# A decoder layer with a sixth raw weight tile, sums and forms placed elsewhere, norm vectors in SyncE's queue, and classical pair steps bank by bank

## The chip, the core and the metric

One core of a Trainium2 chip runs the whole layer. The metric is the device time of one execution in microseconds (us), lower is better. The kernel before has a median of 1880.06 us over three runs (1879.97 to 1880.45).

## The reference, cut to what matters

The layer has 256 rows and a width of 2048, all in float32. Three token mixers read one projection, their outputs are gated and merged, and a SwiGLU block follows.

```python
h = rms_norm(x, g_pre_mix)
proj = h @ w_in                                  # 2048 x 17488, split into 12 parts
o_a = dsa_attention(...)                         # 64 chosen keys of 256
o_b = retention(...)
o_c = memory_attention(..., rms_norm(mem, g_mem) @ w_mem_kv)
mixed = sum over branches of sigmoid(gate) * (o @ w_branch)
x = x + rms_norm(mixed @ w_out, g_post_mix)
h2 = rms_norm(x, g_pre_ffn)
f_gate, f_up = split(h2 @ w_ffn_in)              # 2048 x 11264
x = x + rms_norm((silu(f_gate) * f_up) @ w_ffn_out, g_post_ffn)
```

## The kernel before, in words

**Weights.** Nearly all work is matrix products of 256 rows with weights from HBM. A `Load` is a raw weight tile of 128 x 4 x 512 float32 (1 MB), fetched by SyncE's queue (SP, L427) into a pool `wr` of `Stream.RAWS` = 5 tiles. Each half of it is an `Item`: ScalarE (ACT) rounds it to float32r (`whi`, L432), VectorE (DVE) makes the remainder (`wlo`, L438), and TensorE (PE) multiplies three times: whi with hi, wlo with hi, whi with lo (L507; `hi` and `lo` are the rounded operand and its remainder). A unit of a normal `Job` is 12 such matmuls, all 512 columns wide; two PSUM banks, one for each half of the rows, are written in turn, three matmuls at a time.

**Order.** `Stream.run` writes the order of the whole program by hand, with no scheduler: before each unit s it issues loads whose first item is at most s + 6 (as long as no more than `RAWS` tiles are in use), casts up to s + 3, remainders up to s + 2, and then the unit's matmuls. Each engine runs its own list in the order in which it was written. Evacuations go into a `fast` list, other side work into a `slow` list, and each unit lets one step of each run (`tick`).

**Pairs.** 19 times two neighbouring products with the same operand are done as a `Pair`: 8 in the gates, merges and `w_out`, 8 in the feed-forward block's first product, and 3 chunks of one pair in `w_ffn_out`. A pair replaces some of its products by a Strassen-like step of seven blocks (each one block = 6 matmuls into one bank, half a unit), and does the rest classically. Its steps are written as `152d3ddd6dd7ccc4ccc` (a shorter string in the last chunk): digits are blocks, `c` and `d` are classical units of the first and the second product. The first product has the banks W and X, the second Y and V. Block 7 is written into X, and `take_7` copies it out with the sign turned (ACT, L313; in the second and third chunk DVE, L315) before X is used for the first `c` step, whose matmuls alternate W, X, W, X. Blocks 5, 6, 7 and 4 need weight sums: the first is a DVE addition of two raw tiles (`t1`, L275; a `Sum` that `add_up` places at most 6 items ahead), the others are accumulating transfers on GpSimd's queue (POOL, L271). Blocks with operand sums read `fhi` and `flo`, which `make_forms` makes from hi and lo (its DVE addition `whole`, an ACT cast, and the remainder at L743); for the retention output `ob` it is put into the slow list at the fourth `values` (i == 3).

**Side transfers.** `turned` transposes an activation through HBM: 8 transfers `d<-y` (L681), then one `turned<-d` (L685), all in SP's queue between the weight loads. Norm vectors (`gain`, 128 x 512, the same row on every partition) come by `bcast` on POOL's queue (L1217); `load_x` fetches a part of x on SP, then two gains, which DVE uses at L1234 and L1236. Side tiles come from the pools `tp` (31 tiles of type T) and `hp` (8 of type H).

Of the kernel before, what the change touches and what calls it, by code (L numbers as in the profile page):

```python
# [19 lines left out]
P = 128  # L20
# [130 lines left out]
class Unit:  # L151


    def __init__(self, s, muls, ready, weight=1.0, begin=None, end=None):
        self.s, self.muls, self.ready, self.weight = s, muls, ready, weight
        self.begin, self.end = begin, end


class Stream:


    RAWS = 5

# [94 lines left out]
    def plan_pair(self, pr):  # L258
# [82 lines left out]
        def plain(g, c, hf, ends):  # L341
            l = loads[g, c]
            s = self.add_item([l], 512, lambda: l.half(hf))
            pair = [acc[a] for a in ("WX", "YV")[g]]

            def stat(m):
                return lambda q: [t[c][:, 2 * hf + q, m * P:(m + 1) * P] for t in (xop.hi, xop.lo)]

            def begin():
                for a in pair:  # L350
                    self.begin(a)

            def end():
                for k in ends:
                    finish(k)
            self.add_unit(Unit(s, [(pair[m], stat(m)) for m in range(2)],
                               lambda: all((c, m) in xop.ready for m in range(2)), begin=begin,
                               end=end if ends else None))

# [81 lines left out]
    def run(self, jobs):  # L441
# [4 lines left out]
        where = {id(l): i for i, l in enumerate(loads)}  # L446
        srcs, his, los = [], [], []
        loaded, summed, added, passed = 0, 0, 0, 0.0

        def add_up():  # L450

            nonlocal summed
            if summed == len(self.sums):
                return False
            t = self.sums[summed]
            if t.after >= len(los) or any(where[id(l)] >= loaded for l in t.loads):
                return False
            t.fn()
            summed += 1
            return True  # L460

        for n, unit in enumerate(self.units):
            s = unit.s
            more = True
            while more:
                more = False
                while loaded < len(loads) and loads[loaded].first <= s + 6:
                    if sum(l.last >= len(los) for l in loads[:loaded]) >= (3 if loaded < 8 else self.RAWS):
                        break
                    self.load(loads[loaded], (4, 2, 2, 2)[loaded] if loaded < 4 else 1)  # L470
                    loaded += 1
                while added < len(self.adds) and self.adds[added].after < len(los):
# [22 lines left out]
            if summed < len(self.sums) and self.sums[summed].before <= s + 6:  # L495
                add_up()
            if unit.begin:
                unit.begin()
            self.until(unit.ready)
            hi, lo = his[s], los[s]  # L500
            for q in range(2):
                for a, parts in unit.muls:
                    xh, xl = parts(q)
                    for x, w in ((xh, hi), (xh, lo), (xl, hi)):
                        held = unit.end is not None and q == 1 and w is hi and x is xl
                        a.n += 1
                        PE.matmul(a.tile, x, w[:, q], start=a.n == 1,  # L507
                                  stop=a.n == a.total or held, skip_group_check=a.read)
            if unit.end:
# [10 lines left out]
def tile_layer(ctx: ExitStack, tc: tile.TileContext, io):  # L520
# [3 lines left out]
    const = ctx.enter_context(tc.tile_pool(name="const", bufs=1))  # L524
    tp = ctx.enter_context(tc.tile_pool(name="tp", bufs=31))
    hp = ctx.enter_context(tc.tile_pool(name="hp", bufs=8))
# [284 lines left out]

    def pair(rows=in_T):

        two = jobs.pop()
        jobs.append(Pair(jobs.pop(), two, rows))
# [372 lines left out]
    def values(i):  # L1188
        def evac(ps):
            tmp = []  # L1190
            yield from copied(tmp, "rv", "x")(ps)
            st.slow.append(retain(i, tmp[0]))
            if i == 3:
                st.slow.append(make_forms(ob, 0))
        return evac
# [19 lines left out]
    def bcast(src, i, n="gain"):  # L1215
        t = H([P, 512], n)
        G.dma_start(t, bass.AP(tensor=src.tensor, offset=src.offset + 512 * i, ap=[[0, P], [1, 512]]))  # L1217
        return t
# [177 lines left out]
    def ffn_up(j):  # L1396
        def evac(ps):
            if j == NF - 1:
                st.slow += [make_forms(act, c) for c in (0, 4, 8)]
            t = ffn.pop(j)  # L1400
            for m in range(2):
                V.scalar_tensor_tensor(t[m], ps[m], rmt["ffn", m], t[m], op0=ALU.mult, op1=ALU.mult)
                yield "free" if m else None
            yield
            turned(t, split_turned(act))
        return evac

    for j in range(NF):
        jobs.append(Job(h2, io["w_ffn_in"][2 * j], KD, 512, ffn_gate(j), lead="" if j else "first"))
        jobs.append(Job(h2, io["w_ffn_in"][2 * j + 1], KD, 512, ffn_up(j)))  # L1410
        if j in BLOCKS:
            pair(lambda g: (in_T if g else in_H)(g))

# [9 lines left out]
    def fin_evac(i):  # L1423
        def evac(ps):
            gt = bcast(io["g_post_ffn"], i)
            if i == 1:
                for k in kept:
                    xr.append(T([P, 2, 512], n="xr"))
                    nc.sync.dma_start(xr[-1], k)
                yo3["g"] = bcast(io["g_post_ffn"], 3)  # L1430
            yo3[i] = T([P, 2, 512], n="yo3")
            yield
# [110 lines left out]
```

## Time and profile before

| | |
|---|---|
| median of 3 runs | 1880.06 us (1879.97 to 1880.45) |
| the profiled execution | 1882.16 us, of which the span from first to last instruction is 1880.4 |
| PE, busy | 1861.9 us (99%), 8330 matmuls |
| PEld (PE's weight loads), busy | 1533.2 us (82%) |
| DVE, busy | 1241.9 us (66%) |
| ACT, busy | 938.7 us (50%) |
| POOL, busy | 75.7 us (4%) |
| HBM read | 411 MB, 229 GB/s over the span |

The span is that of the core's instructions; the profiled execution is 1.8 us longer than it, since it also counts what lies before the first and behind the last. PE's busy time is that of overlapping matmuls: one is shown with 0.39 us, while the next starts 0.23 us later. A short wait is therefore read from the distance of two starts, and a wait shown in brackets, which counts from the modelled end, is short by 0.39 - 0.23 = 0.16 us.

### The profile page before, as it was taken

How to read it: one execution, taken by the hardware profiler on the slowest of the kernel's cores; microseconds unless marked ns; L12 is line 12 of the kernel's file. 1: busy time of each engine (PE TensorE's matmuls, PEld its weight loads, DVE VectorE, ACT ScalarE, POOL GpSimd, SP SyncE). 2: the span in 40 equal slices, each digit the busy share in tenths (PEclk: the TensorE clock that was granted, in tenths of full speed). 3: DMA queues.
4: the chain of work that ended last, by engine and by line, in shares of the span. 5: the costliest groups of instructions: out<-in, count | busy, mean ns of one | idle time of the engine just before them, and what ended most of it. 6: DMA issues, size and time to landing. Idle time of an engine off the chain costs nothing.

```text
span 1880.4 us, 21857 instructions
## 1 busy us (share of the span) xinstructions
PE 1861.9 (99%) x8330; PEld 1533.2 (82%) x8330; DVE 1241.9 (66%) x1509; ACT 938.7 (50%) x1111; POOL 75.7 (4%) x98
## 2 busy tenths in 40 slices
PE   9999999999999999999999999999999999999998
PEld 6888878888888888888887887888888888887886
DVE  5766767777656654556777676756767676666664
ACT  7744444545545444444555444545555555445442
POOL 0000000000000000000100000000000000000000
PEclk9999999999999999999999999999999999999999
DMA  9847565547676756555668684578888887577782
GB/s 372 307 164 265 209 241 188 183 177 247 216 243 217 226 207 221 192 196 189 211 218 296 213 280 157 208 233 286 275 272 257 258 248 244 186 262 226 238 291 84
DMA packets 106201, 432.59 MB, mean 230 GB/s; under 512 B 12000, under 2 KB 43232, under 8 KB 64624
## 3 DMA queue, kind: packets, MB, share of 16 engines
q1 hardware_dynamic: 96720, 398.12, 57.3%
q0 software_dynamic: 9232, 33.07, 10.1%
q8 instruction: 65, 1.06, 0.2%
q14 instruction: 40, 0.33, 0.0%
q10 hardware_dynamic: 144, 0.01, 0.0%
HBM read 411.22 MB, written 19.92 MB: 229 GB/s over the span
## 4 chain that ended last, share of the span: by engine, by line
PE 92%; DVE 3%; DMA 2%; issue 2%; ACT 1%; SPq 0%; POOL 0%; POOLq 0%; DVEq 0%; ACTq 0%
PE acc L507 89%; DVE wlo L438 1%; DMA raw<-in_w_mem_kv 1%; DMA gain<-in_g_pre_ffn 0%; DMA gain<-in_g_post_ffn 0%; PE bk L1049 0%; DMA raw<-in_w_in 0%; PE bk L1031 0%; PE bk L923 0%; ACT whi L432 0%; DMA raw<-in_w_out 0%; PE bk L996 0%; DVE y L673 0%; PE bk L1163 0%; PE bk L1016 0%
## 5 line engine op out<-in xcount | busy, mean ns | idle before, releaser
L432 ACT CAST whi<-raw 128x1024 fp32r<-128x1024 f32 (+1 forms) x731 | 759.9, 1043 | 798.1 <-PE acc L507 715.8
L438 DVE TENSOR_TENSOR wlo<-raw,whi 128x1024 fp32r<-128x1024 f32 (+1 forms) x731 | 875.0, 1208 | 329.4 <-ACT whi L432 326.2
L507 PE MATMUL acc<-whi,hi 128*128 128x512 f32 (+2 forms) x2498 | 978.1, 392 | 3.2 <-ACT snap L313 1.9
L507 PE MATMUL acc<-wlo,hi 128*128 128x512 f32 (+2 forms) x2498 | 969.6, 388 | 3.2 <-DVE wlo L438 3.1
L507 PE MATMUL acc<-whi,lo 128*128 128x512 f32 (+2 forms) x2498 | 968.9, 388 | 0.0
L507 PEld LDWEIGHTS acc<-whi,hi 128*128 128x128 f32 x2498 | 469.9, 188 | 106.6 <-ACT snap L313 9.3
L507 PEld LDWEIGHTS acc<-wlo,hi 128*128 128x128 f32 x2498 | 470.0, 188 | 99.3 <-DVE wlo L438 6.5
L507 PEld LDWEIGHTS acc<-whi,lo 128*128 128x128 f32 x2498 | 469.7, 188 | 95.3
L507 PE MATMUL acc<-wlo,fhi 128*128 128x512 f32 x152 | 59.3, 390 | 1.0 <-DVE wlo L438 1.0
L507 PE MATMUL acc<-whi,flo 128*128 128x512 f32 x152 | 59.4, 391 | 0.6 <-DVE flo L743 0.6
L507 PE MATMUL acc<-whi,fhi 128*128 128x512 f32 x152 | 59.7, 393 | 0.0
L384 DVE TENSOR_TENSOR snap<-acc,snap 128x512 f32<-128x512 f32 x38 | 26.2, 689 | 34.0 <-PE acc L507 26.4
L363 DVE TENSOR_TENSOR snap<-acc,snap 128x512 f32<-128x512 f32 x19 | 13.1, 692 | 44.5 <-PE acc L507 44.5
L271 POOL DMA_DIRECT2D raw<-in_w_in x18 | 15.5, 860 | 630.1 <-DMA raw<-in_w_in 423.4
L712 DVE TENSOR_TENSOR lo<-turned,hi 128x1024 fp32r<-128x1024 f32 x16 | 19.6, 1227 | 31.4 <-ACT hi L711 31.3
L507 PEld LDWEIGHTS acc<-wlo,fhi 128*128 128x128 f32 x152 | 28.6, 188 | 7.2 <-DVE wlo L438 1.4
L271 POOL DMA_DIRECT2D raw<-in_w_ffn_in x24 | 20.5, 852 | 342.8 <-DVE wlo L438 268.5
L507 PEld LDWEIGHTS acc<-whi,flo 128*128 128x128 f32 x152 | 28.5, 188 | 6.9 <-DVE flo L743 1.0
L507 PEld LDWEIGHTS acc<-whi,fhi 128*128 128x128 f32 x152 | 28.6, 188 | 5.8
L308 DVE TENSOR_TENSOR snap<-snap,acc 128x512 f32<-128x512 f32 x19 | 13.0, 687 | 30.2 <-PE acc L507 30.2
L275 DVE TENSOR_TENSOR raw<-raw,raw 128x1024 f32<-128x1024 f32 x19 | 23.2, 1221 | 14.7 <-DMA raw<-in_w_in 11.6
L798 DVE TENSOR_TENSOR rp<-acc,cos 128x512 f32<-128x512 f32 (+2 forms) x24 | 14.5, 604 | 20.8 <-PE acc L507 20.8
(197 smaller groups left out, 701.6 us busy)
## 6 DMA issues: line engine op xcount, KB each, us to landing
raw<-in_w_in SPq DMA_DIRECT2D x132, 1024.0 KB, 6.8
raw<-in_w_ffn_in SPq DMA_DIRECT2D x88, 1024.0 KB, 5.6
raw<-in_w_ffn_out SPq DMA_DIRECT2D x44, 1024.0 KB, 6.5
raw<-in_w_branch_b SPq DMA_DIRECT2D x16, 1024.0 KB, 5.3
raw<-in_w_out SPq DMA_DIRECT2D x16, 1024.0 KB, 5.5
d<-y SPq DMA_DIRECT2D x240, 64.0 KB, 1.8
turned<-d SPq DMA_DIRECT2D x30, 512.0 KB, 6.2
raw<-in_w_mem_kv SPq DMA_DIRECT2D x12, 1024.0 KB, 11.9
```

What stands on the lines that cost most here:

```text
L271: return lambda: G.dma_start(l.half(hf).rearrange("p a b -> p (a b)"), pr.jobs[g].w[cs][:, 1024 * k:1024 * k + 1024], accum_op=ALU.add)
L275: V.tensor_add(r2.half(0), r2.half(0), r1.half(0))
L308: V.tensor_sub(row(1, 0), row(1, 0), acc["X"].tile)
L363: V.tensor_add(t, acc["W"].tile, t)
L384: V.tensor_add(row(1, m), acc[a].tile, row(1, m))
L432: self.nc.scalar.copy(hi[:, sl], src[:, sl])
L438: self.nc.vector.tensor_sub(lo[:, sl], src[:, sl], hi[:, sl].bitcast(F32))
L507: PE.matmul(a.tile, x, w[:, q], start=a.n == 1, stop=a.n == a.total or held, skip_group_check=a.read)
L712: V.tensor_sub(l4, v, h4.bitcast(F32))
L798: V.tensor_tensor(t1, s4, cos, op=ALU.mult)
```

## The change

`RAWS` becomes 6 and the loads' look-ahead s + 8, so that each raw load stands one place earlier; the pool `tp` shrinks from 31 to 29 tiles to make room, and the rows that a pair sets aside for its first product (`in_TH`) become one H tile, in place of T tiles (in the feed-forward pairs: of two H tiles). `add_up(4)` places the first sum of a pair only when its two loads were issued at least four units before; the call with no age, just before the sum is needed, stays. `bcast` issues on SP instead of POOL. `make_forms(ob, 0)` is put in at i == 1, and the one for the third chunk of `act` moves out of `ffn_up` into `fin_evac(2)`, 24 ticks later. `by_bank` sorts the matmuls of a pair's classical steps: first all six of one bank, then the six of the other.

```diff
--- before.py
+++ after.py
@@ -151,15 +151,15 @@
 class Unit:
 
 
-    def __init__(self, s, muls, ready, weight=1.0, begin=None, end=None):
-        self.s, self.muls, self.ready, self.weight = s, muls, ready, weight
+    def __init__(self, s, muls, ready, weight=1.0, begin=None, end=None, by_bank=False):
+        self.s, self.muls, self.ready, self.weight, self.by_bank = s, muls, ready, weight, by_bank
         self.begin, self.end = begin, end
 
 
 class Stream:
 
 
-    RAWS = 5
+    RAWS = 6
 
     def __init__(self, nc, wr, ws, acc, nm, T):
         self.nc, self.wr, self.ws, self.acc, self.nm, self.T = nc, wr, ws, acc, nm, T
@@ -355,7 +355,7 @@
                     finish(k)
             self.add_unit(Unit(s, [(pair[m], stat(m)) for m in range(2)],
                                lambda: all((c, m) in xop.ready for m in range(2)), begin=begin,
-                               end=end if ends else None))
+                               end=end if ends else None, by_bank=True))
 
         def finish(g):
             def first():
@@ -444,16 +444,16 @@
         PE = self.nc.tensor
         loads, items = self.loads, self.items
         where = {id(l): i for i, l in enumerate(loads)}
-        srcs, his, los = [], [], []
+        srcs, his, los, since = [], [], [], []
         loaded, summed, added, passed = 0, 0, 0, 0.0
 
-        def add_up():
+        def add_up(age=0):
 
             nonlocal summed
             if summed == len(self.sums):
                 return False
             t = self.sums[summed]
-            if t.after >= len(los) or any(where[id(l)] >= loaded for l in t.loads):
+            if t.after >= len(los) or any(where[id(l)] >= loaded or since[where[id(l)]] > n - age for l in t.loads):
                 return False
             t.fn()
             summed += 1
@@ -464,10 +464,11 @@
             more = True
             while more:
                 more = False
-                while loaded < len(loads) and loads[loaded].first <= s + 6:
+                while loaded < len(loads) and loads[loaded].first <= s + 8:
                     if sum(l.last >= len(los) for l in loads[:loaded]) >= (3 if loaded < 8 else self.RAWS):
                         break
                     self.load(loads[loaded], (4, 2, 2, 2)[loaded] if loaded < 4 else 1)
+                    since.append(n)
                     loaded += 1
                 while added < len(self.adds) and self.adds[added].after < len(los):
                     self.adds[added].fn()
@@ -493,19 +494,21 @@
                         his.append(self.high(srcs[h], it.nw, 2 if h < 2 else 1))
                     more = True
             if summed < len(self.sums) and self.sums[summed].before <= s + 6:
-                add_up()
+                add_up(4)
             if unit.begin:
                 unit.begin()
             self.until(unit.ready)
             hi, lo = his[s], los[s]
-            for q in range(2):
-                for a, parts in unit.muls:
-                    xh, xl = parts(q)
-                    for x, w in ((xh, hi), (xh, lo), (xl, hi)):
-                        held = unit.end is not None and q == 1 and w is hi and x is xl
-                        a.n += 1
-                        PE.matmul(a.tile, x, w[:, q], start=a.n == 1,
-                                  stop=a.n == a.total or held, skip_group_check=a.read)
+            order = [(a, parts, q) for q in range(2) for a, parts in unit.muls]
+            if unit.by_bank:
+                order.sort(key=lambda o: unit.muls.index(o[:2]))
+            for a, parts, q in order:
+                xh, xl = parts(q)
+                for x, w in ((xh, hi), (xh, lo), (xl, hi)):
+                    held = unit.end is not None and q == 1 and w is hi and x is xl
+                    a.n += 1
+                    PE.matmul(a.tile, x, w[:, q], start=a.n == 1,
+                              stop=a.n == a.total or held, skip_group_check=a.read)
             if unit.end:
                 unit.end()
             passed += unit.weight
@@ -522,7 +525,7 @@
     V, A, PE, G = nc.vector, nc.scalar, nc.tensor, nc.gpsimd
 
     const = ctx.enter_context(tc.tile_pool(name="const", bufs=1))
-    tp = ctx.enter_context(tc.tile_pool(name="tp", bufs=31))
+    tp = ctx.enter_context(tc.tile_pool(name="tp", bufs=29))
     hp = ctx.enter_context(tc.tile_pool(name="hp", bufs=8))
     wr = ctx.enter_context(tc.tile_pool(name="wr", bufs=Stream.RAWS))
     ws = ctx.enter_context(tc.tile_pool(name="ws", bufs=4))
@@ -809,7 +812,10 @@
     def in_H(g):
         return [H([P, 512], "snap") for _ in range(2)]
 
-    def pair(rows=in_T):
+    def in_TH(g):
+        return in_T(g) if g else [H([P, 512], "snap")]
+
+    def pair(rows=in_TH):
 
         two = jobs.pop()
         jobs.append(Pair(jobs.pop(), two, rows))
@@ -1190,7 +1196,7 @@
             tmp = []
             yield from copied(tmp, "rv", "x")(ps)
             st.slow.append(retain(i, tmp[0]))
-            if i == 3:
+            if i == 1:
                 st.slow.append(make_forms(ob, 0))
         return evac
 
@@ -1214,7 +1220,7 @@
 
     def bcast(src, i, n="gain"):
         t = H([P, 512], n)
-        G.dma_start(t, bass.AP(tensor=src.tensor, offset=src.offset + 512 * i, ap=[[0, P], [1, 512]]))
+        nc.sync.dma_start(t, bass.AP(tensor=src.tensor, offset=src.offset + 512 * i, ap=[[0, P], [1, 512]]))
         return t
 
     xr, xg, yg, ygg, heads = [], [], [], [], []
@@ -1396,7 +1402,7 @@
     def ffn_up(j):
         def evac(ps):
             if j == NF - 1:
-                st.slow += [make_forms(act, c) for c in (0, 4, 8)]
+                st.slow += [make_forms(act, c) for c in (0, 4)]
             t = ffn.pop(j)
             for m in range(2):
                 V.scalar_tensor_tensor(t[m], ps[m], rmt["ffn", m], t[m], op0=ALU.mult, op1=ALU.mult)
@@ -1409,7 +1415,7 @@
         jobs.append(Job(h2, io["w_ffn_in"][2 * j], KD, 512, ffn_gate(j), lead="" if j else "first"))
         jobs.append(Job(h2, io["w_ffn_in"][2 * j + 1], KD, 512, ffn_up(j)))
         if j in BLOCKS:
-            pair(lambda g: (in_T if g else in_H)(g))
+            pair()
 
 
     ssq3 = const.tile([P, 2, 4], F32, name="ssq3")
@@ -1428,6 +1434,8 @@
                     xr.append(T([P, 2, 512], n="xr"))
                     nc.sync.dma_start(xr[-1], k)
                 yo3["g"] = bcast(io["g_post_ffn"], 3)
+            if i == 2:
+                st.call(24, lambda: st.slow.append(make_forms(act, 8)))
             yo3[i] = T([P, 2, 512], n="yo3")
             yield
             for m in range(2):
```

PE's order at the end of block 7 and in the first `c` step behind it, in the first pair (gates of branch a, about 470 us); `acc_4316` is bank X, `acc_4344` bank W, and the wait on ACT at the first matmul of X in the `c` step is the one for `take_7`. Before:

```order
L507 MATMUL acc_4316<-whi_4433,flo_3712 128x512
L507 MATMUL acc_4344<-whi_4444,hi_535 128x512 [waits Activation_49]
L507 MATMUL acc_4344<-wlo_4462,hi_535 128x512 [waits DVE_49]
L507 MATMUL acc_4344<-whi_4444,lo_536 128x512
L507 MATMUL acc_4316<-whi_4444,hi_535 128x512 [waits Activation_49]
L507 MATMUL acc_4316<-wlo_4462,hi_535 128x512
L507 MATMUL acc_4316<-whi_4444,lo_536 128x512
L507 MATMUL acc_4344<-whi_4444,hi_535 128x512
```

With the change (`acc_4346` is now W):

```order
L510 MATMUL acc_4316<-whi_4433,flo_3713 128x512
L510 MATMUL acc_4346<-whi_4446,hi_537 128x512 [waits Activation_49]
L510 MATMUL acc_4346<-wlo_4464,hi_537 128x512 [waits DVE_49]
L510 MATMUL acc_4346<-whi_4446,lo_538 128x512
L510 MATMUL acc_4346<-whi_4446,hi_537 128x512
L510 MATMUL acc_4346<-wlo_4464,hi_537 128x512
L510 MATMUL acc_4346<-whi_4446,lo_538 128x512
L510 MATMUL acc_4316<-whi_4446,hi_537 128x512 [waits Activation_49]
```

The first matmul into X, with the wait, stands three matmuls later; the three of W take its place.

SP's order around one `turned` in the second pair of the gates of branch b (about 984 to 1005 us); `d_7795` and `d_7797` are the transfers `d<-y` of the same activation. Before:

```order
L685 DMA turned_7753<-d_7655 128x1024 [waits DMAHW5_49,DMAHW4_49,DMAHW6_49,DMAHW1_49,DMAHW7_49,DMAHW0_49,PE_49]
L427 DMA raw_7773<-in_w_in 128x2048 [waits DVE_49]
L681 DMA d_7795<-y_7792 32x4x128 [waits DVE_49] x2
L681 DMA d_7795<-y_7792 32x4x128 x2
L681 DMA d_7795<-y_7792 32x4x128 [waits DMAHW2_49]
L681 DMA d_7795<-y_7792 32x4x128 [waits DMAHW3_49]
L681 DMA d_7795<-y_7792 32x4x128 [waits DMAHW4_49]
L681 DMA d_7795<-y_7792 32x4x128 [waits DMAHW5_49]
L427 DMA raw_7826<-in_w_in 128x2048 [waits DMAHW6_49,Activation_49]
L427 DMA raw_7876<-in_w_in 128x2048 [waits DMAHW7_49,Activation_49]
```

With the change:

```order
L427 DMA raw_7743<-in_w_in 128x2048 [waits DMAHW4_49,Activation_49]
L688 DMA turned_7755<-d_7657 128x1024 [waits DMAHW5_49,DMAHW2_49,DMAHW6_49,DMAHW1_49,DMAHW7_49,DMAHW0_49,PE_49]
L427 DMA raw_7775<-in_w_in 128x2048 [waits DVE_49]
L684 DMA d_7797<-y_7794 32x4x128 [waits DVE_49] x2
L684 DMA d_7797<-y_7794 32x4x128 x2
L684 DMA d_7797<-y_7794 32x4x128 [waits DMAHW3_49]
L684 DMA d_7797<-y_7794 32x4x128 [waits DMAHW4_49]
L684 DMA d_7797<-y_7794 32x4x128 [waits DMAHW5_49]
L684 DMA d_7797<-y_7794 32x4x128 [waits DMAHW6_49]
L427 DMA raw_7839<-in_w_in 128x2048 [waits DMAHW7_49,Activation_49]
```

`raw_7775` is the tile that is `raw_7826` before: it stands ahead of the 8 transfers `d<-y` now, and so does every tile by one place.

The norm vectors for `w_out`. Before, on POOL, with the accumulating transfers (L271) between them:

```order
L1217 DMA gain_8238<-in_g_post_mix 128x512 [waits DMASW7_49,PE_49]
L1217 DMA gain_8240<-in_g_pre_ffn 128x512 [waits DMASW0_49,PE_49]
L271 DMA raw_8215<-in_w_out 128x1024 [waits DMAHW5_49,DMAHW2_49,DMAHW7_49,DMAHW1_49,DVE_49]
L1217 DMA gain_8330<-in_g_post_mix 128x512 [waits DMASW2_49,PE_49]
L1217 DMA gain_8332<-in_g_pre_ffn 128x512 [waits DMASW3_49,PE_49]
L271 DMA raw_8215<-in_w_out 128x1024 [waits DVE_49]
L271 DMA raw_8215<-in_w_out 128x1024 [waits DMASW5_49,DMASW1_49,DVE_49]
```

With the change they stand on SP, behind the part of x that goes with them:

```order
L427 DMA raw_8217<-in_w_out 128x2048 [waits DMAHW5_49,DVE_49]
L1234 DMA xr_8237<-in_x 128x2x512
L1223 DMA gain_8239<-in_g_post_mix 128x512
L1223 DMA gain_8241<-in_g_pre_ffn 128x512 [waits DMAHW6_49]
L427 DMA raw_8291<-in_w_out 128x2048 [waits DMAHW7_49,DVE_49]
L1234 DMA xr_8330<-in_x 128x2x512 [waits DMAHW0_49,PE_49]
L1223 DMA gain_8332<-in_g_post_mix 128x512 [waits DMAHW1_49]
L1223 DMA gain_8334<-in_g_pre_ffn 128x512 [waits DMAHW2_49]
L427 DMA raw_8350<-in_w_out 128x2048 [waits DMAHW3_49,DVE_49]
```

POOL's queue is left with the accumulating transfers there; SP's has two transfers of 256 KB more behind each `xr`, ahead of the next weight tiles.

## Rows read from the trace of the kernel before

**Rows 1.** Page, part 1: busy time of each engine, share of the span, instructions

```profile
PE 1861.9 (99%) x8330; PEld 1533.2 (82%) x8330; DVE 1241.9 (66%) x1509; ACT 938.7 (50%) x1111; POOL 75.7 (4%) x98
```

**Rows 2.** Waits of PE's weight loads: us in total, times, longest us

```profile
PEld acc L507 <- ACT snap L313: 9.3, 17, 2.4
PEld acc L507 <- DVE wlo L438: 7.9, 12, 1.4
...
PEld acc L507 <- DVE snap L315: 1.0, 2, 0.5
```

**Rows 3.** Timeline at the first pair: start us, us, engine, line, [idle before <-releaser]

```profile
470.05 0.60 ACT L313 ACTIVATE snap<-acc 128x512 f32<-128x512 f32 x1 [0.30 <-PE acc L507]
...
470.30 0.39 PE L507 MATMUL acc<-whi,lo 128*128 128x512 f32 x1
...
470.70 0.50 PE L507 MATMUL acc<-whi,hi 128*128 128x512 f32 x1
...
471.04 0.39 PE L507 MATMUL acc<-wlo,hi 128*128 128x512 f32 x1
...
471.27 0.40 PE L507 MATMUL acc<-whi,lo 128*128 128x512 f32 x1
```

**Rows 4.** Timeline at the longest wait, ACT and PE

```profile
1005.82 1.04 ACT L432 CAST whi<-raw 128x1024 fp32r<-128x1024 f32 x1 [4.02 <-DVE wlo L438]
1006.77 0.59 ACT L313 ACTIVATE snap<-acc 128x512 f32<-128x512 f32 x1
...
1007.42 0.50 PE L507 MATMUL acc<-whi,hi 128*128 128x512 f32 x1 [1.95 <-ACT snap L313]
```

**Rows 5.** Timeline of SP's queue, 970 to 1000 us

```profile
984.65 0.42 SPq L427 DMA_DIRECT2D raw<-in_w_in  x1
993.13 5.56 SPq L681 DMA_DIRECT2D d<-y  x8
998.79 0.42 SPq L427 DMA_DIRECT2D raw<-in_w_in  x1
```

**Rows 6.** Windows behind that wait: us, busy by engine, PEclk, DMA share, GB/s

```profile
1008.00:1012.00 4.00, 4.00 (x12) 3.15 (x11) 3.49 (x4) 2.87 (x5) 0.00 (x0) 0.57 1.03 433
```

**Rows 7.** Timelines of SP, DVE and PE, 855 to 885 us

```profile
870.18 3.84 SPq L681 DMA_DIRECT2D d<-y  x8
...
881.61 1.23 DVE L275 TENSOR_TENSOR raw<-raw,raw 128x1024 f32<-128x1024 f32 x1 [6.92 <-DMA raw<-in_w_in]
...
884.03 0.50 PE L507 MATMUL acc<-wlo,hi 128*128 128x512 f32 x1 [0.59 <-DVE wlo L438]
```

**Rows 8.** Timeline of PE at 939 us

```profile
939.36 0.50 PE L507 MATMUL acc<-whi,flo 128*128 128x512 f32 x1 [0.56 <-DVE flo L743]
```

**Rows 9.** Timelines of POOL, DVE and PE, 1068 to 1080 us

```profile
1068.69 0.88 POOL L271 DMA_DIRECT2D raw<-in_w_out  x1 [73.95 <-DVE wlo L438]
...
1078.18 0.69 DVE L1234 TENSOR_TENSOR xg<-xr,gain 128x512 f32<-128x512 f32 x1 [2.14 <-DMA gain<-in_g_pre_ffn]
...
1080.07 0.50 PE L507 MATMUL acc<-wlo,hi 128*128 128x512 f32 x1 [0.90 <-DVE wlo L438]
```

**Rows 10.** Timelines of POOL and PE, 1692 to 1703 us

```profile
1692.16 0.87 POOL L1217 DMA_DIRECT2D gain<-in_g_post_ffn  x1
...
1702.38 0.51 PE L507 MATMUL acc<-wlo,fhi 128*128 128x512 f32 x1 [0.98 <-DVE wlo L438]
```

**Rows 11.** Timeline of DVE around a first sum in the feed-forward block

```profile
1237.73 1.22 DVE L275 TENSOR_TENSOR raw<-raw,raw 128x1024 f32<-128x1024 f32 x1
...
1244.29 1.23 DVE L438 TENSOR_TENSOR wlo<-raw,whi 128x1024 fp32r<-128x1024 f32 x1 [1.54 <-ACT whi L432]
```

**Rows 12.** Timelines of SP and ACT, 1097 to 1119 us

```profile
1100.26 8.36 SPq L427 DMA_DIRECT2D raw<-in_w_out  x3
...
1101.43 0.62 ACT L1249 ACTIVATE junk<-snap 128x512 f32<-128x512 f32 x1
...
1118.19 1.05 ACT L432 CAST whi<-raw 128x1024 fp32r<-128x1024 f32 x1 [1.09 <-issue]
```

## The prediction

> **What bounds the kernel now.** I read the busy times first: PE is busy 99% of the span, the other engines 66% or less [rows 1]. So time is to be had in two ways only: fewer matmuls, or the small waits between them. The change keeps every matmul, so I go through the waits. The view of waits shows three groups for PE's weight loads that bear on the change: 17 times the copy at L313, 12 times a remainder `wlo`, twice the DVE copy at L315 [rows 2]. Their totals count the weight load, which runs ahead of the matmul, so they overstate; what PE loses I take from the distance of two matmul starts. Undisturbed it is 0.23 us, as from 471.04 to 471.27 [rows 3]. Where a matmul row has a wait in brackets, the loss is that wait plus 0.16 us (0.39 shown less the 0.23 pitch).
>
> In every wait the matmul behind also starts late: 0.34 us after the first one in place of 0.23 [rows 3], so 0.11 us more is lost per wait. I add this each time.
>
> **Part 1: the classical steps bank by bank.** After block 7 the copy at L313 reads bank X from 470.05 to 470.65; the first matmul into X starts at 470.70, 0.40 us after the one before it [rows 3]. Loss: 0.40 - 0.23 + 0.11 = 0.28 us. The view of waits counts 17 such; one of them is the 2.4 us of part 2, the other 16 share 9.3 - 2.4 = 6.9 us, 0.43 each in the weight load [rows 2], so they are alike. With X behind six matmuls of W in place of three, X is needed 3 x 0.23 = 0.69 us later. The copy ends 0.05 us before 470.70, and X was due at 470.53; three matmuls later that is 471.22, and the copy is done 0.57 us ahead. All 16 go: 16 x 0.28 = 4.5 us. The sort itself costs nothing that I can find: blocks already put six matmuls into one bank at the 0.23 us pitch. What could be late next is a reader of W, but no copy reads W there.
>
> The two waits for L315 in `w_ffn_out` are 1.0 us in the weight load together [rows 2]; in the ratio above (0.43 there for 0.28 on PE) some 0.35 us each. One goes likewise. In the other the operand sum that is now made during the second chunk (1.2 us on DVE, as the addition of the same size at L275 [rows 7]) may stand ahead of the copy, and eat the 0.69 us: I leave it. Part 1 gives 4.5 + 0.35 = 4.9 us.
>
> **Part 2: the sixth raw tile, where a weight load came late.** The longest wait of PE ends at 1007.42, lost 1.95 + 0.16 + 0.11 = 2.2 us [rows 4]. It names L313 again, but that copy only stood behind a cast that started at 1005.82 after 4.02 us idle. DVE, which is named there, is not the cause; it is the raw tile, issued at 998.79 behind the 8 transfers `d<-y` that hold SP's queue from 993.13 [rows 5]. Then the granted clock falls: 0.57 over 1008 to 1012 us [rows 6], between the levels of 2.4 and 1.2 GHz; PE lost 4.00 x (1 - 0.57) = 1.7 us there. With the change this tile is issued ahead of the `d<-y`, in the place of the load at 984.65, 14 us earlier [rows 5]; even if its buffer came free only just ahead of 993.13 it would be 5.7 us earlier. The cast then starts without those 4.02 us of idle time, and the copy need not stand behind it. X was due at 1007.42 - 1.95 - 0.16 = 1005.31; block 7 ended about four matmuls before that, by 1004.8, and a copy of 0.59 us [rows 4] ends by 1005.4. By part 1's order X is due at 1006.0. The gap goes, and the lower clock with it, since PE waits nowhere else there: 3.9 us.
>
> The same at 884: the first sum of the pair (L275) sat 6.92 us for a raw tile that was issued behind `d<-y` (870.18 to 874.02), and held the remainder behind it; PE lost 0.59 + 0.16 + 0.11 = 0.86 us [rows 7]. That tile moves ahead of them too, and the sum may be placed only four units after its loads, two remainders later: 0.86 us.
>
> **Part 3: forms of `ob`.** At 939.36 PE waits for `flo`: 0.56 + 0.16 + 0.11 = 0.83 us [rows 8]. The forms are now made two `values` earlier, in a stretch of normal jobs, where a remainder is made up to two items ahead of its unit; the DVE's work of 1.2 us and less at a time [as L275, rows 7] lies beside matmuls there. If that cover were gone the same 0.83 us would come back. I count 0.83 us.
>
> **Part 4: norm vectors on SP.** At 1080.07 PE loses 0.90 + 0.16 + 0.11 = 1.17 us to a remainder, which stood behind the multiplication at 1078.18 that had waited 2.14 us for a gain [rows 9]. The gain was issued on POOL behind an accumulating transfer that had held that queue for 73.95 us, until 1068.69 [rows 9]. On SP it stands right behind its part of x, with no accumulating transfer ahead of it, and x was there when the multiplication came: so is the gain, one or two issues later, 0.4 us each by the load at 984.65 [rows 5]. The same pattern at 1702.38, where the gain was issued on POOL at 1692.16 behind such a transfer: 0.98 + 0.16 + 0.11 = 1.25 us [rows 10]. Part 4 gives 2.4 us.
>
> A page of the Trainium skill speaks against this. "DMA: Bandwidth & Descriptors", section "Issuing engines are not separate DMA queues", says that transfers of all issuing engines run on the same 16 DMA engines, and that moving the issue saves only the time to initiate them. By that alone part 4 would be worth one issue on POOL, 0.87 us [rows 10], and the sum 1.5 us less. The trace shows that what held these gains was neither transfer nor issue but the order of one queue [rows 9], so I don't follow it here.
>
> **What is added.** (a) First sums come later. At 1237.73 one stands in DVE's list [rows 11]; two remainders later it falls into an idle stretch such as the 1.54 us before 1244.29 [rows 11], where its 1.22 us fit. Cost bounds: 0 if it fits, 1.22 + 0.11 us a pair if a remainder that PE waits for stands right behind. I take 0, the nearest row being that stretch. (b) Two new waits in SP's queue: the gains of the third and fourth part of `w_out` take H tiles that ACT wrote as `junk`, the first until 1101.43 + 0.62 = 1102.05; behind it in SP's queue the load issued at 1100.26 would go out 1.8 us later [rows 12]. That tile is cast at 1118.19, 18 us after its issue [rows 12], so 1.8 us are covered: cost 0. With the cover gone it is up to 1.8 us for each of the two. (c) Two T tiles fewer and one more transfer in flight: no engine waits longer for a tile that I can find, cost 0, and up to 1 us if one does.
>
> **Sum.** 4.9 + 3.9 + 0.86 + 0.83 + 2.4 = 12.9 us; I take 12.8, since the remaining L315 wait can grow by 0.1. The durations are of the execution of 1882.16 us, 2.1 us above the median; that becomes 1869.4, and from the median 1880.06 - 12.8 = **1867.3 us**. Its own range is 1865.5 to 1869.5: the other 9 waits for a remainder, some 4 us at the weight load [rows 2], may shrink with the earlier loads, and each term can keep a part.
>
> **Rivals.**
> A. The copy is late all the same: W is written by six matmuls, but the second wait or a slower start of X keeps the 0.28 us. For it: the wait is the same in all 16 pairs, like a fixed cost. Against: the copy ends 0.05 us before PE goes on, each time. Then 12.8 - 4.5 = 8.3 us: 1871.8.
> B. The stall at 1007 only shrinks and moves, with the lower clock behind it, since SP's queue is as full with the six tiles: half of 3.9 stays, or all: 1869.3 to 1871.2.
> C. Nothing is gained: each wait repaired gives way to the next late piece (DVE behind the sums, PE's other waits), as PE is 99% busy and what is left is 1%: 1879 to 1880. Against: the six waits have five different causes.
> D. Slower. The later sums hold up DVE in all 19 pairs: the sum is behind a cast and before the remainder that PE needs next, as at 881.61, where it cost 0.86 us [rows 7]. It decides from where the idle stretch is shorter than the sum's 1.22 us; at 0.86 to 1.33 us for 19 pairs, 16 to 25 us are added, near 21 in the middle: 1867.3 + 21 = 1888. For it: DVE has only 1.54 us of idle time between remainders there [rows 11], of which the sum takes 1.22. Against: the earlier sums stood between such remainders too, and PE did not wait.
> E. The gains are late on SP too, queued with weight loads, and part 4 brings only the one issue on POOL, 0.87 us [rows 10] in place of 2.4: 12.8 - 1.5 = 11.3 us, 1868.8. Against: POOL's 73.95 us [rows 9] are no transfer. The section of the skill named in part 4 speaks for it.
>
> **Chances.** Forecast 0.63, A 0.13, B 0.07, C 0.07, D 0.06, E 0.04. A measurement of this kernel can tell about 0.2% (3.8 us) from no change. Faster by more (below 1876.3): forecast, A, B and E, 0.87; within it: C, 0.07; slower: D, 0.06. The range 1863.8 to 1873.0 holds the forecast, E, B and A; C and D are left out. Its lower end is the forecast less 3.5 of those 4 us of other waits; the upper one is A with another 1.2 us of B.
>
> **What the profile after would show.** PE busy time about the same, 8330 matmuls, and a span some 13 us shorter. Part 1: no or few waits of PE's weight loads for L313, and rows of X behind six of W at the 0.23 us pitch. Part 2: granted clock 1.00 around 1000 us, casts without a long idle time there, and the sum of 881 with no wait for a transfer. Part 3: no wait for `flo`. Part 4: no gains in POOL's list and no DVE idle time named after one. The prediction is wrong if waits for L313 stay at 0.28 us of distance each (A), if a half clock turns up elsewhere (B), or if remainders behind L275 make PE wait in many pairs (D).

## The result, and the profile after

The changed kernel takes 1868.95 us (median of 4 runs, 1868.81 to 1873.04), the one before 1880.01 beside it: a ratio of 0.9947, 95% interval [0.9929, 0.9964]. Measured again, with 5 and 17 runs, it was 1868.89 to 1881.25, ratio 0.9934 [0.9922, 0.9947]. So it is 11 to 12 us faster. The forecast was 1867.3 with a range of 1863.8 to 1873.0. Two slow runs, of 5399 and 2327 us, are left out of the medians in the experiments e1 and e2.

The page of the changed kernel, busy times and (below) waits of PE's weight loads, which answer to [rows 1, 2]:

```profile
span 1866.9 us, 21860 instructions
PE 1852.6 (99%) x8330; PEld 1532.9 (82%) x8330; DVE 1242.7 (67%) x1509; ACT 938.8 (50%) x1111; POOL 69.0 (4%) x86
```

```profile
PEld acc L510 <- DVE wlo L438: 3.9, 8, 1.1
PEld bk L929 <- PE acc L510: 2.8, 8, 0.4
PEld acc L510 <- ACT whi L432: 2.4, 2, 1.4
```

The same 8330 matmuls; no wait for L313, L315 or `flo` is left (L929 is a product inside the attention, the same as before). PE's busy time is 9 us less with the same work: waits too short to be shown as idle, and the slow matmuls behind 1008 us, counted as busy. The timeline at the first pair shows why part 1 worked, against [rows 3]:

```profile
469.77 0.60 ACT L313 ACTIVATE snap<-acc 128x512 f32<-128x512 f32 x1 [0.30 <-PE acc L510]
...
470.02 0.39 PE L510 MATMUL acc<-whi,lo 128*128 128x512 f32 x1
470.25 0.39 PE L510 MATMUL acc<-whi,hi 128*128 128x512 f32 x1
470.48 0.39 PE L510 MATMUL acc<-wlo,hi 128*128 128x512 f32 x1
470.70 0.39 PE L510 MATMUL acc<-whi,lo 128*128 128x512 f32 x1
470.93 0.39 PE L510 MATMUL acc<-whi,hi 128*128 128x512 f32 x1
```

The copy ends at 470.37; the matmul at 470.25 is the fourth of W, and X is first written at 470.93, 0.56 us after the copy. The pitch is 0.23 us throughout.

SP's queue and ACT at the place of [rows 4, 5], and the granted clock that answers to [rows 6]:

```profile
982.38 0.70 SPq L427 DMA_DIRECT2D raw<-in_w_in  x1
987.99 8.35 SPq L684 DMA_DIRECT2D d<-y  x8
997.00 0.35 SPq L427 DMA_DIRECT2D raw<-in_w_in  x1
```

```profile
999.65 1.06 ACT L432 CAST whi<-raw 128x1024 fp32r<-128x1024 f32 x1 [1.71 <-PE acc L510]
1000.97 0.60 ACT L313 ACTIVATE snap<-acc 128x512 f32<-128x512 f32 x1 [0.26 <-PE acc L510]
```

```profile
999.00:1003.00 4.00, 4.00 (x19) 3.34 (x18) 3.97 (x6) 3.09 (x4) 0.00 (x0) 1.00 1.01 424
```

The cast waits for PE now (a free buffer), not for a tile; the copy follows block 7 at once. At the place of [rows 7] the sum has its tiles, and at that of [rows 9] the gains were issued 30 us before their use:

```profile
878.54 1.22 DVE L275 TENSOR_TENSOR raw<-raw,raw 128x1024 f32<-128x1024 f32 x1
```

```profile
1038.93 0.56 SPq L1223 DMA_DIRECT2D gain<-in_g_pre_ffn  x1
```

```profile
1068.25 0.68 DVE L1240 TENSOR_TENSOR xg<-xr,gain 128x512 f32<-128x512 f32 x1
```

I laid the 8330 matmul starts of the two profiles side by side. PE is ahead by 1.5 us after the four pairs up to 663, by 2.4 after 884, 3.5 after 939, 3.9 after 963, 7.6 after 1011, 8.9 after 1081, 11.7 after 1574, 12.9 after 1703, and 14.1 us at the last matmul. The span is only 13.5 us shorter: from the start of the last matmul to its end it takes 9.14 us, against 8.55 before.

### The profile page after: what moved, and what is told of

Same layout as the page of the kernel before. It is cut to its first block, busy times and chain, and to the rows that moved or that the text cites. A ratio compares the mean times of both kernels' runs of the same rounds, so it can differ in the third digit from the quotient of the medians.

```text
span 1866.9 us, 21860 instructions
## 1 busy us (share of the span) xinstructions
PE 1852.6 (99%) x8330; PEld 1532.9 (82%) x8330; DVE 1242.7 (67%) x1509; ACT 938.8 (50%) x1111; POOL 69.0 (4%) x86
## 4 chain that ended last, share of the span: by engine, by line
PE 97%; DVE 1%; DMA 1%; issue 1%; ACT 0%; POOL 0%; SPq 0%; POOLq 0%; DVEq 0%
PE acc L510 94%; DMA raw<-in_w_mem_kv 1%; DVE wlo L438 0%; PE bk L1055 0%; PE bk L1037 0%; PE bk L929 0%; PE bk L1002 0%; PE bk L1022 0%; PE bk L1168 0%; PE bk L1155 0%; PE bk L1167 0%; PE bk L1169 0%; PE bk L1011 0%; PE bk L661 0%; DVE rp L802 0%
## 5 line engine op out<-in xcount | busy, mean ns | idle before, releaser
L271 POOL DMA_DIRECT2D raw<-in_w_in x18 | 15.5, 860 | 626.4 <-DVE wlo L438 620.9
L363 DVE TENSOR_TENSOR snap<-acc,snap 128x512 f32<-128x512 f32 x19 | 13.1, 692 | 31.6 <-PE acc L510 31.6
L271 POOL DMA_DIRECT2D raw<-in_w_ffn_in x24 | 20.4, 850 | 341.0 <-DVE wlo L438 334.4
L1106 DVE TENSOR_TENSOR gate<-gate,acc 128x512 f32<-128x512 f32 x21 | 14.4, 684 | 23.5 <-PE acc L510 23.5
```

Source lines behind the costliest of these rows:

```text
L271: return lambda: G.dma_start(l.half(hf).rearrange("p a b -> p (a b)"), pr.jobs[g].w[cs][:, 1024 * k:1024 * k + 1024], accum_op=ALU.add)
L363: V.tensor_add(t, acc["W"].tile, t)
L1106: V.tensor_tensor(g[:, m], g[:, m], ps[m], op=ALU.mult)
```

## The experiments

Steps of PE's start against another kernel's profile, matmul by matmul, are given as "on PE". The labels e1 to e10 name the runs.

**The order by banks alone (e1)**, on the kernel before, with the sort of the change:

```diff
-                               end=end if ends else None))
+                               end=end if ends else None, by_bank=True))
```

> The kernel before with one part of the change alone: classical steps of a pair bank by bank. My theory (the 17 + 2 waits are the copy's, and X is due 0.69 us later): no waits for L313 at the 16 places, about 0.28 us of distance gone at each, 0.35 at the two of L315, and the wait at 1007 us shrinks by 0.69 us: 1880.0 - 4.5 - 0.7 - 0.7 = 1874.1, or 1872.4 if the clock does not fall behind the shorter wait. Rival A (a fixed cost of X's first matmul): 0.28 us of distance stays behind the six matmuls of W, about 1879.3. Rival F (the 2.1 us by which the profiled execution of before lay above the median of its runs is the stretch of lower clock at 1008 us, which the other executions did not have): the timed runs gain no more than 5.9 us, while the profile may show 7.6.

Measured: ratio 0.9963 [0.9950, 0.9977], median 1873.6 (1872.33 to 1877.10 in four runs), 6.8 us less, between my two numbers. On PE: 0.19 + 0.11 = 0.30 us at each of the 16 places, 0.40 at both places of L315. Rival A is out. Most of the wait of [rows 10] was gone too (0.2 us left), though the gain stands on POOL as before: it landed in 7.1 us, against 8.2 in the first profile. That of [rows 9] was 0.8 us shorter, with its gain landing in 7.5 us in place of 8.4. Two more things came along. At 939 us 0.70 us of the wait for `flo` went, though the forms stand where they stood; DVE in e1:

```profile
934.63 0.69 DVE L363 TENSOR_TENSOR snap<-acc,snap 128x512 f32<-128x512 f32 x1
935.24 1.22 DVE L438 TENSOR_TENSOR wlo<-raw,whi 128x1024 fp32r<-128x1024 f32 x1
936.37 1.22 DVE L745 TENSOR_TENSOR flo<-whole,fhi 128x1024 fp32r<-128x1024 f32 x1
```

L363 reads bank W at the end of the pair. With W's matmuls first it is complete three matmuls (0.69 us) earlier, and all that follows on DVE moves up. And the long wait is still there, 1.50 us, with the clock at 1.00 behind it:

```profile
1005.63 0.50 PE L509 MATMUL acc<-whi,hi 128*128 128x512 f32 x1 [1.50 <-ACT snap L313]
```

```profile
1004.00:1008.00 4.00, 2.50 (x11) 1.97 (x11) 2.39 (x3) 3.96 (x6) 0.00 (x0) 1.00 1.01 422
1008.00:1012.00 4.00, 4.00 (x19) 3.29 (x19) 2.84 (x3) 3.54 (x5) 0.00 (x0) 1.00 0.94 348
```

**The raw tile and the sums (e3)**, without banks, gains and forms of `ob` (lines against the changed kernel, cut short):

```diff
-                               end=end if ends else None, by_bank=True))
+                               end=end if ends else None))
-        nc.sync.dma_start(t, bass.AP(tensor=src.tensor,
+        G.dma_start(t, bass.AP(tensor=src.tensor,
-            if i == 1:
+            if i == 3:
                 st.slow.append(make_forms(ob, 0))
```

> The kernel before with the sixth raw tile, the look-ahead of 8, the later first sums, and the form sum of the third chunk moved, but without the order by banks, with the norm vectors on GpSimd's queue and the forms of ob at i == 3. My theory: the waits at 884 us (0.86) and 1007 us (2.2) go, and the lower clock behind the latter (1.7): 1880.0 - 4.8 = 1875.2, with the 16 waits of 0.28 us for L313 in place, as well as those for flo and the gains. Rival B (the stall only shrinks and moves): 1877 to 1878.5. Rival F (the lower clock is not in most executions of before): 1880.0 - 3.1 = 1876.9. Rival D (later sums hold up DVE): above 1880.

Measured: ratio 0.9985 [0.9977, 0.9994], median 1877.45 to 1880.42, 3.0 us. That is rival F's number and not mine, although the profile against the first one of before shows both places repaired (0.86 at 884, 1.88 and 1.5 of clock at 1007). The third chunk lost 0.8 us at L315, where the form sum stands ahead of the copy. The gains are on POOL here too, and yet PE loses nothing at 1702 and only 0.5 us at 1080: they landed in 6.95 and 7.7 us. DVE at the place of [rows 10], in e3 and then in e8 (gain landed in 8.2 us, PE lost 1.2); the wait for the gain is 1.2 us longer in e8:

```profile
1696.01 0.69 DVE L1427 TENSOR_TENSOR yo<-acc,gain 128x512 f32<-128x512 f32 x1 [2.43 <-DMA gain<-in_g_post_ffn]
```

```profile
1691.08 0.69 DVE L1427 TENSOR_TENSOR yo<-acc,gain 128x512 f32<-128x512 f32 x1 [3.64 <-DMA gain<-in_g_post_ffn]
```

**The gains alone (e4)**, on the kernel before (lines cut short):

```diff
-        G.dma_start(t, bass.AP(
+        nc.sync.dma_start(t, bass.AP(
```

> The kernel before with the norm vectors issued in SyncE's queue alone. My theory: the waits at 1080 (1.17 us) and 1702 us (1.25) go: 1880.0 - 2.4 = 1877.6. Rival E (only the issue is saved): 1879.1. Rival G (gains ahead of weight loads in SyncE's queue make those late): a new idle stretch of ACT behind a load between 1040 and 1120 us, and 1880 or more.

Measured: ratio 0.9989 [0.9980, 0.9998], median 1878.56, 1.9 us less. On PE 1.15 at 1080 and 1.13 + 0.15 at 1702: 2.4 us. The times alone (interval 0.4 to 3.8 us) don't tell this from rival E's 0.9; the profile does. Rival G is out: PE loses nothing between 1040 and 1120 us. The wait at 1007, which this edit doesn't touch, lost 1.94 us too, and its lower clock. Against that, 1.9 us more were lost at 138 us and 0.8 at 1572, where a cast stood ahead of the copy; why it came late there stays open.

**The kernel before, once more (b_again).**

> The kernel before, unchanged, profiled a second time. Theory F (the profiled execution of before that the prediction rests on lay high, because waits behind weight transfers differ from one execution to the next): the 16 waits for L313 stand there again with 0.28 us each, as does the one for flo, but the wait at 1007 us is shorter than 2.1 us or has no lower clock behind it, and the whole is at or below the median of 1880.4. Theory S (the same in every execution, and the 2 us lie outside of the span): the same waits within 0.1 us, the clock at 0.57 over 1008 to 1012 us again, span 1880.4.

Measured: 1880.32, ratio 0.9995 [0.9986, 1.0004]; the profiled run 1880.88. PE and ACT at the place of [rows 4], and the window of [rows 6]:

```profile
1007.80 0.50 PE L507 MATMUL acc<-whi,hi 128*128 128x512 f32 x1 [0.38 <-ACT snap L313]
```

```profile
1006.20 1.06 ACT L432 CAST whi<-raw 128x1024 fp32r<-128x1024 f32 x1 [2.44 <-DVE whole L737]
1007.15 0.59 ACT L313 ACTIVATE snap<-acc 128x512 f32<-128x512 f32 x1
```

```profile
1008.00:1012.00 4.00, 4.00 (x18) 3.29 (x18) 4.00 (x5) 3.91 (x5) 0.00 (x0) 1.00 1.04 435
```

0.38 + 0.16 + 0.11 = 0.65 us in place of 3.9. In exchange 1.3 us more were lost at 138 us, where a weight tile took 8.32 us to land, and 0.4 more at 884. The waits for L313 and `flo`, which hang on no transfer, agree to 0.1 us. Theory F holds.

**The changed kernel, once more (a_again).**

> The changed kernel, unchanged, profiled a second time. Theory F: the waits for a raw tile at the start of the kernel and near 137 us differ by up to 2 us from the first profile, the rest of PE's starts agree to 0.3 us; the runs spread over 3 us or more as those of before do, and the median over more runs lies above 1868.9, at 1869.5 to 1871. Theory S: 1868.9 within 0.5, and the same starts throughout.

Measured: 1868.89 (1868.55 to 1870.00). From 13 us on all of PE's starts agree with the first profile within 0.15 us. F's wider spread did not show in these five runs, which lie within 1.5 us; but one of the first four had 1873.04. Whether the earlier loads make the spread smaller is not shown: e3 has them too, and its 11 runs spread over 3.3 us, the 11 of b_again over 3.7.

**The changed kernel without the order by banks (e2)**, twice (the diff is the first two lines of the second experiment).

> The changed kernel without the order by banks. My theory: the waits for L313 come back, 0.28 us of distance at 17 places, and for L315 0.4 at two or more, with the sum of 1.2 us on DVE ahead of one of them at 1750 us, so 1.2 there: +4.8 + 0.4 + 1.2 = 6.4 over the changed kernel run beside it (1875.3 from 1868.9). Rival A (fixed cost): no more than +1.

> The changed kernel without the order by banks, for its profile at full clock (the first one was taken at a mean granted clock of 0.752). It ran 7.3 us above the changed kernel, 0.9 more than the 6.4 I had worked out. My theory: 17 waits for L313 of 0.28 us (4.8), and the two places of L315 cost 2.5 together, most of it at 1750 us, where the operand sum of 1.2 us stands ahead of the copy on DVE. Rival (other small waits appear with the order of banks, as at the gates): the two L315 places cost 1.6 or less, and the rest is elsewhere.

Measured: 1876.16, 7.3 us above the changed kernel beside it, with ratio 0.9972 [0.9961, 0.9983] to before; the second time 1876.89, 0.9980 [0.9971, 0.9989]. The second profile: 17 waits for L313, 0.30 each on PE (5.1), and L315 cost 1.27 + 0.40 more. DVE and PE at the larger one:

```profile
1757.74 1.22 DVE L734 TENSOR_TENSOR whole<-hi,lo 128x1024 f32<-128x1024 f32 x1
1758.87 1.22 DVE L438 TENSOR_TENSOR wlo<-raw,whi 128x1024 fp32r<-128x1024 f32 x1
1760.01 0.68 DVE L315 TENSOR_TENSOR snap<-snap,acc 128x512 f32<-128x512 f32 x1
```

```profile
1759.43 0.39 PE L510 MATMUL acc<-whi,lo 128*128 128x512 f32 x1
1760.74 0.50 PE L510 MATMUL acc<-whi,hi 128*128 128x512 f32 x1 [0.93 <-DVE snap L315]
```

The form sum pushes the copy back; in the changed kernel the same sum stands there, and the 0.69 us hide it. These make 6.8 of 7.3; the rest stays open (my theory's split, 2.5 for L315, was too much). This profiled run, at 1880.43, lay 3.5 above its median. A `turned` landed after 13.06 us and PE waited 2.4, with a clock of 0.76 behind:

```profile
983.79 13.06 DMA turned<-d
```

```profile
1001.63 0.50 PE L510 MATMUL acc<-wlo,hi 128*128 128x512 f32 x1 [2.40 <-DVE wlo L438]
```

```profile
1004.00:1008.00 4.00, 4.00 (x14) 2.91 (x12) 3.73 (x6) 1.63 (x3) 0.00 (x0) 0.76 0.99 413
```

**Look-ahead back to 6, six tiles kept (e7); and the same without the age (e10).**

```diff
-                while loaded < len(loads) and loads[loaded].first <= s + 8:
+                while loaded < len(loads) and loads[loaded].first <= s + 6:
```

> The changed kernel with the look-ahead set back from 8 to 6 items, six raw tiles kept. In SyncE's list the weight loads then stand behind the transfers of a transpose again, as in the kernel before. My theory (the earlier place in the queue is what removed the stall, not the sixth tile as such): the wait near 1000 us comes back, 1.4 us long as X is due 0.69 us later, with 0.11 behind it, and 1.7 more if the clock falls: 1868.9 + 1.5 to 3.2 = 1870.4 to 1872.1. The wait of 884 us stays away, as the sum now stands behind the remainder. Rival (the sixth tile alone does it): 1868.9 and no wait there.

Measured: 1877.35, 8.5 us above the changed kernel: far more than I expected. The profiled run, at 1875.77, was the lowest of 11; in it new waits came at 441 (1.5 us on PE), 888 (1.0), 1002 (1.6), 1065 (0.7) and 1785 us (1.5). The view of waits of this run has a row that the changed kernel has once (1.3 us):

```profile
ACT whi L432 <- DVE raw L275: 45.6, 17, 4.1
```

```diff
-                add_up(4)
+                add_up()
```

> The changed kernel with the look-ahead of 6 and the first sums placed with no age: loads and sums stand as before the change, while the order by banks, the places of the gains and of the forms stay. The kernel with a look-ahead of 6 alone ran at 1877.4, 8.5 us above the changed one and 5 above what I had expected. Theory L (the age rule holds a sum back when its loads are late: it is then placed at the last moment, and its cast is written behind other work of ACT, as at 441 us): without the age the waits at 441, 888, 1064 and 1785 us go, and 1870 to 1872 is left, the waits at 884 and 1002 us in it. Rival (late loads cost that much in any case): 1875 to 1878.

Measured: 1871.79 (1870.84 to 1873.18), ratio 0.9954 [0.9941, 0.9968], 2.9 us above 1868.9. Theory L holds: with late loads and the age, first sums come at the last moment, and casts wait for them in 17 pairs. Without the age only the wait of [rows 7] is back:

```profile
881.00 1.23 DVE L275 TENSOR_TENSOR raw<-raw,raw 128x1024 f32<-128x1024 f32 x1 [7.03 <-DMA raw<-in_w_in]
```

```profile
883.42 0.50 PE L510 MATMUL acc<-wlo,hi 128*128 128x512 f32 x1 [0.69 <-DVE wlo L438]
```

0.96 us. The wait at 1007 was not there in this profile; X's 0.69 us later would cover the 0.65 of b_again. So this run does not show that the earlier loads are what removes it.

**The age alone taken out (e6)** (look-ahead 8, the edit just above).

> The changed kernel with first sums placed as early as before (no age asked for), loads one place earlier kept. My theory (earlier loads are enough, the sum of 884 us finds its tile): within 1 us of the changed kernel. Rival D2 (the later place is needed: a sum right behind the issue of its loads holds VectorE until they land): idle time of DVE ahead of L275 named after a raw tile at several pairs, and 0.3 to 0.9 us of PE for each, +1 to +6 us.

Measured: 1869.40 (1868.67 to 1869.77), 0.5 us above the changed kernel beside it; on PE the difference is 0.7 us and all of it before 15 us, elsewhere none. No DVE idle time stands ahead of L275. So the age gains nothing here. The wait of 884 is gone with the earlier loads alone (here) and with the age alone (e7); either would have done.

**The gains back on POOL (e8), and the forms back at i == 3 (e5)**, each on the changed kernel (the diffs are lines of the second experiment).

> The changed kernel with the norm vectors back in GpSimd's queue. My theory (part 4 of the prediction, order of the queue): the waits near 1071 and 1690 us come back, 1.2 us each, +2.4 on the changed kernel run beside it (1868.9 to 1871.3). Rival E (only the issue): +0.9 or less. Theory F (what a wait behind a transfer costs differs from one execution to the next): the wait near 1690 is there in some executions only, and the median is +1.2 to +2.4 with a spread over 1.5 us.

> The changed kernel with the forms of ob put in at the fourth values (i == 3) again. My theory: the wait for flo near 936 us comes back, +0.83 us on the changed kernel. Rival: X's later place in the pair's order and the earlier casts leave room, so that it stays hidden: 0.

Measured: 1871.74 (1869.20 to 1872.58), ratio to before 0.9949 [0.9937, 0.9962], and 1869.47 (1868.78 to 1870.77), 0.9941 [0.9929, 0.9953]. On PE the gains cost 0.73 at 1071 and 1.22 at 1690, so 1.95 us; the median is 2.8 above 1868.9, the runs 0.3 to 3.7. The profiled run is the median one: of its 3.6 us on PE another 1.2 were lost before 140 us, where no gain is fetched, and 0.3 at 997, while the end of the program takes 8.56 us again, 0.6 less. The forms cost 0.17 us, not 0.83.

## Why the prediction was right, and where not

What PE lost at five places, in us against the first profile of the changed kernel; in parentheses, how long after its issue on POOL the gain landed:

| profile | 138 us | 884 | 1007 | 1080 | 1702 |
|---|---|---|---|---|---|
| before | 0.3 | 0.9 | 3.9 | 1.2 (8.4) | 1.3 (8.2) |
| b_again | 1.6 | 1.3 | 0.7 | 1.3 (8.4) | 1.2 (8.1) |
| e1 | 0.4 | 1.1 | 1.8 | 0.4 (7.5) | 0.2 (7.1) |
| e4 (gains on SP) | 2.2 | 1.2 | 0.3 | 0 | 0 |
| e3 | 0.9 | 0 | 0.6 | 0.5 (7.7) | 0 (6.9) |
| e8 | 0.7 | 0 | 0.3 | 0.7 (7.9) | 1.2 (8.2) |

**Part 1 right, a little small.** 4.9 forecast; on PE in e1 about 5.6: each place gave 0.30, and both L315 waits went. I left one of them in for fear of the form sum; the 0.69 us hide that.

**Part 2 is the term that was mis-sized.** "The gap goes, and the lower clock with it, since PE waits nowhere else there: 3.9 us" is true of the one execution that I read. The loss at 1007 was 0.3 to 3.9 us in the four profiles whose loads stand as before (outside of e1, 0.3 of it is the plain L313 wait), with a lower clock in one of them. That a raw tile held the cast, and not DVE, holds: in before, b_again and e1 the cast starts 0.10 us after its tile landed (at 1005.72, 1006.10 and 1003.94), while DVE had ended 0.02 to 0.26 us earlier than the cast began. But against b_again e3, which has the earlier loads, gains only 0.1 us there, and they don't rule such a stall out: in e2's second profile, which has them too, PE lost 4.3 us near 1000 behind the late `turned`. The wait of 884 us was a lasting one: 0.86 forecast, 0.9 to 1.3 in those four, 0.96 in e10.

**Part 3 right in its sum, not in its cause.** The 0.83 us went whole. But the order by banks alone takes 0.70 of it, by giving W back earlier; beside it, the forms' place is worth 0.17 (e5). What it is worth by itself was not run.

**Part 4 right in its path, sized from a high execution.** 2.4 forecast; 2.4 on PE in e4, 1.95 in e8. Neither wait stands in a profile with the gains on SP (that of e7 at 1065 is gone without the age, in e10). With them on POOL the loss follows the landing, as the table shows, and in e1 and e3 the two together cost 0.5 to 0.6 us: the queue's order makes the gain late, and how late it lands decides the price. The Trainium skill ("DMA: Bandwidth & Descriptors", "Issuing engines are not separate DMA queues") says that starting transfers from several engines saves only the time to start them. Here the move was worth more in e4 and e8 than rival E's 0.87 us, since the gain no longer stood behind another transfer's wait.

**The added parts cost nothing in PE's stream, as forecast.** The offsets have no step back at 1100 to 1125, where SP waits for H tiles. The later sums hold up nothing (rival D is out); but they don't gain anything either, and with later loads they cost 5.6 us (e7 against e10; 5.2 on PE).

**One cost has no term in the prediction.** From the start of the last matmul to the end of the span it takes 8.55 or 8.56 us in all five profiles with the gains on POOL, 8.78 in e4, and 9.13 to 9.18 in the seven of the changed kernel and its variants with the gains on SP. e8 differs from the changed kernel by the gains alone, so their move costs 0.6 us there; why stays open.

**The sum.** 12.8 off the profiled 1882.16 is 1869.4, 0.5 from what came. Taking the same 12.8 off the median was the step that was off: the profiled execution lay 2.1 us above it, and 3.9 of the 12.8 stood in that execution only. That the forecast still came near is in part luck. Against b_again PE gains 12.8 us with quite other terms: 4.9 at the 16 places, 0.8 at L315, 0.7 at 1007, 1.3 at 884, 0.8 for `flo`, 2.4 for the gains, and 1.6 at 138 and 0.3 at the start, which the prediction has not. Less the 0.6 at the end and 0.2 outside of the span, that is the 12.0 us between the two runs (1880.88 and 1868.90). So a loss at 138 that I had not counted took the place of most of the 3.9 that I had. Whether the change removes it is not shown: e3 and e8 have the earlier loads and lose 0.9 and 0.7 there, the two profiles of the changed kernel nothing.

Not tried: the smaller T pool, the H tile for pairs and the later form sum of the third chunk by themselves, and the longer look-ahead with five tiles, so the sixth tile's own share is not shown.

## What to carry to other kernels

A copy that reads a bank and the matmuls that write it again need distance: put the other bank's whole work between them, and look at who else reads that bank, since it comes free earlier too. Before a wait behind a transfer is counted, read it in a second execution, since its size goes with the landing, and take the sum off the execution that it was read from. A longer look-ahead and a rule that holds work back until loads are old belong together: the second without the first costs more than both bring.

## What the runs showed of the hardware

The same transfer in the same place lands at quite different times: the `turned` of 512 KB issued at 981 to 986 us took 13.06 us in e2's second profile, 13.58 in e7, 9.65 and 10.12 in the two of the changed kernel, and 7.9 to 8.2 in the four with five raw tiles. The gain of [rows 10], 256 KB, took 6.95 to 8.24 us in five profiles. PE's granted clock dropped behind waits of 1.95 us (0.57 over 1008 to 1012 us) and 2.40 us (0.76 over 1004 to 1008 us), and not behind one of 1.50 us; in 13 profiles these are the only two drops between 15 us and the last matmul.
